# A two-layer diffusion trunk: the modulation sums of one stage moved to VectorE alone and cut into pieces of 512 columns

## The chip, the cores and the metric

One core of one Trainium2 chip. The metric is the device time of one execution in microseconds (us), the median of several runs. The whole program is one launch.

## The reference

Two layers of one trunk over 512 latent tokens (x) and 256 context tokens (ctx), 1024 channels wide. Each layer is a half step of SwiGLU, a token mixer, and a second half step of SwiGLU; each of the three is modulated by vectors that come from a conditioning vector c (for the latents) or c_ctx (for the context). Cut to what matters here:

```python
sc, scc = silu(c), silu(c_ctx)                       # 1024 numbers each
for li in range(2):
    m  = split(sc  @ ada_w[li] + ada_b[li], 9)       # nine vectors of 1024 for the latents
    mc = split(scc @ ada_w[li] + ada_b[li], 9)       # nine for the context
    h  = half_ffn(h,  norm_g[li, 0], m[0],  m[1],  m[2],  ffn_w_gu[li, 0], ffn_w_down[li, 0])
    hc = half_ffn(hc, norm_g[li, 0], mc[0], mc[1], mc[2], ffn_w_gu[li, 0], ffn_w_down[li, 0])
    ...
```

with half_ffn(h, g, shift, scale, gate, w_gu, w_down) = h + 0.5 * gate * swiglu(rms_norm(h, g) * (1 + scale) + shift). The part in question is the product of the two rows sc and scc with ada_w[1], a matrix of 1024 x 9216: the eighteen vectors of layer 1.

## The kernel before, in words

Activations lie transposed, channels on the 128 partitions: h is eight chunks (KC = 8) of 128 channels by 768 tokens. Every matrix product runs on TensorE in fp32r, with weights and activations split into a high and a low part (names ending in h and l) and three matmuls for each product. The stages follow one another: first half step of layer 0, even mixer, second half step of layer 0, first half step of layer 1, odd mixer, second half step of layer 1.

A half step (ffn, line 913) goes through 22 chunks of 128 hidden channels. For a chunk, chain (line 658) multiplies gate and up weights with all channels, for the 512 latent tokens and then for the 256 context tokens, into PSUM banks gb; ScalarE takes the silu (sg), VectorE multiplies (a<-sg,gb), and a is split into a high part (a cast, on ScalarE as a rule) and a low part (a<-a,a on VectorE). After every second chunk comes a down block (out_block, line 672): it multiplies the two chunks with the down weights into bank_c, bank_d and bank_e in turn, and for each of eight output chunks VectorE adds the result to h (h<-bank_c,mod,h). So the second half step of layer 0 is a row of gate/up stretches of two chunks with down blocks between them. Weights come by DMA into raw and are split: the high part w0h to w3h on ScalarE or VectorE, the low part w0l to w3l on VectorE or GpSimd, by whoever is free in the plan.

The modulation vectors of layer 1 are made beside that stage (class Ada, line 839). For one of nine vectors and for each kc of eight, 128 rows by 1024 columns of ada_w are loaded into araw (three buffers; the next load is put on SyncE's queue when the plan has the buffer read). Each row is scaled by its element of silu(c) or silu(c_ctx), a number for each partition, and added into aacc, of 2 x 1024 columns, one half for each of the two. In job (line 859) VectorE does the first half by itself, one scalar_tensor_tensor of 1024 columns; for the second half ScalarE forms the product (amul) and GpSimd adds it. Then sixteen small fp32 matmuls on TensorE against pick, the row sums, add up the 128 partitions of aacc into bank_f, and finish (line 885) copies them out (asb), transposes them with TensorE and adds ada_b into mods. aacc has one buffer, so that the next vector can't begin before the row sums have read it.

What sets the order. Each engine runs its instructions in the order in which the program issues them, and a planner decides this order when the program is built. It keeps a clock for each engine (Machine), which an instruction moves ahead by a cost formula (line 156): for VectorE 67 + 1.17 n ns for a scalar_tensor_tensor over n columns, for GpSimd 100 + 2.2 n. Side jobs are generators on lanes n, m, s, t, a, b and g; what a job yields is the time from which its next part may be issued, a number of ns from the plan's present, or sched.at(...) (line 218): when the named tiles are ready, less slack, and not before the clock of an engine, less lead. The present is TensorE's clock. Between groups of matmuls, tick (line 255) issues all parts whose time has come. In the down blocks of this stage tick is called for the lanes n and m alone, except with the last part (line 684). The modulation jobs run on lane b, from the start of the stage:

```python
for v in range(9):
    sch.add("b", ada.job(1, v, ADA_GAP), 6000.0)     # line 1794; ADA_GAP = 2500.0
```

After each kc job waits ADA_GAP ns, and before each it waits for VectorE's clock to have come to the present. Ahead of chunk 19 of 22 (line 947) the plan waits until lane b is empty, since the space of aacc is lent to weights from there on:

```python
if both and (kind, i) == ("gu", NFF - 3):
    sch.wait_for(lambda: not sch.lanes["b"])
```

The same job runs with seven vectors of layer 0 in the very first stage; the change doesn't touch those.

Of the kernel before, what the change touches and what calls it, by code (L numbers as in the profile page):

```python
# [7 lines left out]
F32 = mybir.dt.float32  # L8
# [3 lines left out]
ALU = mybir.AluOpType  # L12
AXX = mybir.AxisListType.X

D = 1024
KC = 8
# [13 lines left out]
ADA_GAP = 2500.0  # L30
# [34 lines left out]
class Machine:  # L65
# [23 lines left out]
    def rows(self, ap):  # L89

        name = ap.tensor.name
        if name not in self.mem:
            rows, key = [], getattr(ap.tensor, "cap_key", None)
            if key is not None:
                past = self.past.setdefault(key, [])
                bufs = ap.tensor.tag_meta.bufs or 1
                if len(past) >= bufs:
                    rows.append([0, 1 << 30, 0, 128, 0.0, "", self.last(past[-bufs])])
                past.append(name)
            self.mem[name] = rows  # L100
        if ap.space != bass.MemoryType.SB:
            return self.mem[name], (0, 1 << 30, 0, 128)
        step, parts = ap.ap[0]
        p0, lo = divmod(ap.offset, step) if step else (0, ap.offset)
        hi = lo + 1
        for st, n in ap.ap[1:]:
            if st > 0:
                hi += st * (n - 1)
            else:
                lo += st * (n - 1)  # L110
        return self.mem[name], (lo, hi, p0, p0 + parts)
# [196 lines left out]
def trunk(ctx, tc, t, out, stop=None, dbg=None):  # L308
    nc = Machine(tc.nc)
    sch = Sched(nc)  # L310
# [14 lines left out]
    st = const.tile([128, KC, 32], F32, name="st")  # L325
# [513 lines left out]
    class Ada:  # L839
# [11 lines left out]
        def load(self):  # L851
            if self.at < len(self.todo):
# [3 lines left out]
                nc.sync.dma_start(out=raw, in_=t["ada_w"][li, 128 * kc:128 * kc + 128, D * vec:D * vec + D])  # L856
                self.raws.append(raw)

        def job(self, li, vec, gap):

            acc = self.pool.tile([128, 2, D], F32, tag="aacc", name="aacc")
            for kc in range(KC):
                while not self.raws:
                    yield 100.0
                yield sch.at(self.raws[:1], eng="dve")
                raw = self.raws.pop(0)
                s0, s1 = st[:, kc, 0:1], st[:, kc, 1:2]
                if kc == 0:
                    nc.vector.tensor_scalar_mul(acc[:, 0], raw, s0)
                    nc.scalar.mul(acc[:, 1], raw, s1)  # L870
                else:
                    nc.vector.scalar_tensor_tensor(out=acc[:, 0], in0=raw, scalar=s0, in1=acc[:, 0], op0=ALU.mult, op1=ALU.add)
                    m = self.pool.tile([128, D], F32, tag="amul", name="amul", bufs=1)
                    nc.scalar.mul(m, raw, s1)
                    nc.gpsimd.tensor_tensor(out=acc[:, 1], in0=acc[:, 1], in1=m, op=ALU.add)
                sch.later(sch.at([], [raw]), self.load)
                yield gap
            yield sch.at([acc])
            for v in range(2):
                for j in range(4):  # L880
                    nc.tensor.matmul(bank_f[32 * j:32 * j + 32, 0:256], pick[:, v], acc[:, v, 256 * j:256 * j + 256],
                                     start=(v == 0), stop=(v == 1))
            yield from self.finish(li, vec)
# [295 lines left out]
    def ffn_alloc(pool):  # L1179
        def alloc(kind, grp, k=0):  # L1180
            t0, n, _ = grp
            if kind in ("acc", "pen", "last"):
                return pool.tile([128, n], F32, tag=f"{kind}{t0}", name=kind)
            if kind == "rs":
                return pool.tile([128, n], F32, tag=f"rs{t0}", name=kind)
            if kind == "u":
                return pool.tile([128, D], F32, tag="araw", name="u", bufs=3)[:, 0:n]
            return pool.tile([128, TX], F32, tag="sq", name=kind, bufs=3)[:, 0:n]
        return alloc
# [5 lines left out]
    def ffn_rooms():  # L1195
        return {0: (bank_e, bank_f[:, 0:16]), 512: (gb[3], bank_f[:, 16:32])}


    with tc.manual_schedule():
# [15 lines left out]
        ada = Ada(fp, [(0, (2, 3, 4, 5, 6, 7, 8))], 3)  # L1215
# [575 lines left out]
        ada = Ada(fp, [(1, tuple(range(9)))], 3)  # L1791
        ada.fill()
        for v in range(9):
            sch.add("b", ada.job(1, v, ADA_GAP), 6000.0)
        n3 = Norm(1, 0, ffn_alloc(fp), ffn_rooms())
        ffn(fp, gb, 0, 1, [XG, CG], n3, early)
        if stop == "ffn01":
# [360 lines left out]
```

## Time and profile before

| | |
|---|---|
| median of three runs | 2685.04 us (2680.67 to 2686.91) |
| the profiled execution, its own time | 2681.97 us |
| its span, first to last instruction | 2680.2 us |
| mean granted TensorE clock | 0.987 of full speed |
| TensorE matmuls, busy | 2596.9 us, 97% of the span |
| VectorE busy | 1858.7 us, 69% |
| ScalarE busy | 824.9 us, 31% |
| GpSimd busy | 737.9 us, 28% |
| DMA | 249.33 MB, mean 93 GB/s |

The times of engines are from one execution, by the hardware profiler. PE is TensorE (PEld its weight loads), DVE VectorE, ACT ScalarE, POOL GpSimd, SP SyncE, which issues most DMAs. In a row of the timeline stand the start and the length in us, the engine, the line, the operation, the tile written and those read, and a count where several were merged; in brackets the idle time of the engine ahead of it and what ended that. All instructions carry line 198, that of a helper, so that tiles tell them apart. Matmuls are pipelined: one shown with 0.39 us may start 0.23 us behind the last.

### The profile page before, as it was taken

The page shows a single profiled execution, that of the slowest core. Times are in us where ns is not written, and L with a number is a line of the kernel's source. Part 1 is how long each engine was busy: PE and PEld are TensorE (multiplying, and loading weights), DVE is VectorE, ACT ScalarE, POOL GpSimd, SP SyncE. Part 2 cuts the span into 40 slices and gives each one's busy share as a digit, 9 for nine tenths or more (in the row PEclk, how much of TensorE's full clock was granted, in tenths as well). Part 3 has the DMA queues.
Part 4 walks back from the last instruction along what each step waited for, and adds up shares of the span by engine and source line. Part 5 has one row for each costly group of instructions (what it writes and reads, how often), then busy time and mean ns, then how long its engine had stood idle before and what let it go on. Part 6 is the DMA issues. An engine that isn't in the chain of part 4 may idle for free.

```text
span 2680.2 us, 38122 instructions
## 1 busy us (share of the span) xinstructions
PE 2596.9 (97%) x15498; PEld 2254.8 (84%) x15498; DVE 1858.7 (69%) x2727; ACT 824.9 (31%) x1365; POOL 737.9 (28%) x481
## 2 busy tenths in 40 slices
PE   7999999999999889999999999999999999899999
PEld 6888888888777678888888889999997887888887
DVE  6888875456666677788875688787876667655554
ACT  4332321123434432332331433232334333311111
POOL 2453541013433342444441201010113443200000
PEclk9999999999999989999999999999998999899999
DMA  9544542212111144444442113121321212233332
GB/s 270 150 149 126 157 134 63 71 48 79 35 34 27 48 134 125 146 147 133 142 144 68 56 32 95 56 87 48 92 73 36 68 53 66 63 95 95 95 95 87
DMA packets 286922, 249.33 MB, mean 93 GB/s; under 512 B 26178, under 2 KB 256026, under 8 KB 286746
## 3 DMA queue, kind: packets, MB, share of 16 engines
q1 hardware_dynamic: 286378, 246.81, 31.2%
q8 instruction: 121, 1.98, 0.3%
q14 instruction: 55, 0.45, 0.1%
q10 hardware_dynamic: 176, 0.07, 0.0%
q0 software_dynamic: 192, 0.01, 0.0%
HBM read 244.73 MB, written 2.13 MB: 92 GB/s over the span
## 4 chain that ended last, share of the span: by engine, by line
PE 88%; DVE 6%; ACT 2%; issue 1%; DMA 1%; POOL 1%; SPq 0%; ACTq 0%; DVEq 0%; POOLq 0%
PE gb L198 46%; PE bank_c L198 14%; PE bank_d L198 13%; PE bank_e L198 10%; PE bank_f L198 3%; PE S L198 1%; DVE a L198 1%; DVE zl L198 1%; PE Sx L198 1%; PE TB L198 1%; DVE h L198 0%; DVE aacc L198 0%; SPq L198 0%; ACT zh L198 0%; POOL aacc L198 0%
## 5 line engine op out<-in xcount | busy, mean ns | idle before, releaser
L198 POOL TENSOR_TENSOR aacc<-aacc,amul 128x1024 f32<-128x1024 f32 x112 | 309.3, 2762 | 298.8 <-ACT amul L198 287.3
L198 DVE TENSOR_TENSOR a<-sg,gb 128x512 f32<-128x512 f32 (+1 forms) x112 | 64.0, 572 | 303.1 <-PE gb L198 302.6
L198 DVE SCALAR_TENSOR_TENSOR aacc<-araw,st,aacc 128x1024 f32<-128x1024 f32 x112 | 234.1, 2091 | 2.2 <-DMA araw<-in_ada_w 0.2
L198 DVE SCALAR_TENSOR_TENSOR h<-bank_c,mod,h 128x512 f32<-128x512 f32 (+1 forms) x237 | 151.0, 637 | 70.6 <-PE bank_c L198 70.3
L198 DVE SCALAR_TENSOR_TENSOR h<-bank_d,mod,h 128x512 f32<-128x512 f32 (+1 forms) x234 | 148.8, 636 | 69.8 <-PE bank_d L198 69.4
L198 PE MATMUL gb<-zh,w1h 128*128 128x512 f32 (+2 forms) x520 | 175.3, 345 | 0.0
L198 ACT ACTIVATE amul<-araw,st 128x1024 f32<-128x1024 f32 x112 | 128.8, 1150 | 148.1 <-POOL aacc L198 130.6
L198 PE MATMUL gb<-zh,w1l 128*128 128x512 f32 (+2 forms) x512 | 171.7, 342 | 0.0
L198 PE MATMUL gb<-zh,w3h 128*128 128x512 f32 (+2 forms) x504 | 169.0, 344 | 0.0
L198 PE MATMUL gb<-zl,w1h 128*128 128x512 f32 (+2 forms) x488 | 167.2, 343 | 0.0
L198 PE MATMUL gb<-zh,w0l 128*128 128x512 f32 (+2 forms) x496 | 165.4, 343 | 0.0
L198 PE MATMUL gb<-zh,w2l 128*128 128x512 f32 (+2 forms) x488 | 162.9, 344 | 0.0
L198 PE MATMUL gb<-zh,w3l 128*128 128x512 f32 (+2 forms) x480 | 162.2, 344 | 0.0
L198 PE MATMUL gb<-zl,w3h 128*128 128x512 f32 (+2 forms) x468 | 161.1, 344 | 0.0
L198 PE MATMUL gb<-zh,w0h 128*128 128x512 f32 (+2 forms) x472 | 160.9, 348 | 0.0
L198 PE MATMUL gb<-zh,w2h 128*128 128x512 f32 (+2 forms) x472 | 159.5, 346 | 0.0
L198 PE MATMUL gb<-zl,w0h 128*128 128x512 f32 (+2 forms) x444 | 153.5, 346 | 0.1
L198 ACT CAST a<-a 128x512 fp32r<-128x512 f32 (+1 forms) x115 | 61.1, 532 | 295.2 <-DVE a L198 295.0
L198 PE MATMUL gb<-zl,w2h 128*128 128x512 f32 (+2 forms) x440 | 151.8, 345 | 0.0
L198 DVE SCALAR_TENSOR_TENSOR h<-bank_e,mod,h 128x512 f32<-128x512 f32 (+1 forms) x185 | 117.6, 636 | 47.2 <-PE bank_e L198 47.2
L198 ACT ACTIVATE sg<-gb 128x512 f32<-128x512 f32 (+1 forms) x112 | 56.3, 502 | 283.1 <-PE gb L198 283.1
L198 POOL TENSOR_TENSOR u<-u,p 128x384 f32<-128x384 f32 x19 | 23.7, 1250 | 426.1 <-ACT p L198 426.1
(685 smaller groups left out, 7255.7 us busy)
## 6 DMA issues: line engine op xcount, KB each, us to landing
raw<-in_ffn_w_gu SPq DMA_DIRECT2D x176, 512.0 KB, 4.1
araw<-in_ada_w SPq DMA_DIRECT2D x134, 512.0 KB, 3.8
raw<-in_ffn_w_down SPq DMA_DIRECT2D x88, 512.0 KB, 3.7
raw<-in_od_w_in SPq DMA_DIRECT2D x16, 512.0 KB, 4.1
raw<-in_ev_w_in SPq DMA_DIRECT2D x10, 512.0 KB, 3.8
raw<-in_od_w_out SPq DMA_DIRECT2D x8, 512.0 KB, 3.8
xt<-in_ada_w SPq DMA_DIRECT2D x6, 512.0 KB, 7.3
xt<-in_x SPq DMA_DIRECT2D x4, 512.0 KB, 5.4
```

What stands on the lines that cost most here:

```text
L198: return real(*args, **kw)
```

## The change

Class Ada gets a second generator, own, and the row sums at the end of job become a generator of their own, rows, which both use. In own VectorE sums both halves of aacc, in pieces of 512 columns, four for each kc: the scalar for each partition times araw, added to aacc (for kc = 0 the product alone). After each piece the job yields until VectorE's clock in the plan is less than 600 ns ahead; the wait ahead of each kc has a lead of 300 ns; the gap behind each kc is 0.6 x 2500 = 1500 ns. The row sums are issued when the plan's end of the sums lies 2000 ns back (slack = -2000). The nine jobs of layer 1 use own; those of layer 0 keep job.

```diff
+        def own(self, li, vec, gap):
+
+            acc = self.pool.tile([128, 2, D], F32, tag="aacc", name="aacc")
+            for kc in range(KC):
+                while not self.raws:
+                    yield 100.0
+                yield sch.at(self.raws[:1], eng="dve", lead=300.0)
+                raw = self.raws.pop(0)
+                for v in range(2):
+                    for half in (slice(0, D // 2), slice(D // 2, D)):
+                        s1, o, i = st[:, kc, v:v + 1], acc[:, v, half], raw[:, half]
+                        if kc == 0:
+                            nc.vector.tensor_scalar_mul(o, i, s1)
+                        else:
+                            nc.vector.scalar_tensor_tensor(out=o, in0=i, scalar=s1, in1=o, op0=ALU.mult, op1=ALU.add)
+                        yield sch.at([], eng="dve", lead=600.0)
+                sch.later(sch.at([], [raw]), self.load)
+                yield gap
+            yield sch.at([acc], slack=-2000.0)
+            yield from self.rows(li, vec, acc)
+
         def job(self, li, vec, gap):
...
             yield sch.at([acc])
+            yield from self.rows(li, vec, acc)
+
+        def rows(self, li, vec, acc):
             for v in range(2):
                 for j in range(4):
                     nc.tensor.matmul(bank_f[32 * j:32 * j + 32, 0:256], pick[:, v], acc[:, v, 256 * j:256 * j + 256],
...
         for v in range(9):
-            sch.add("b", ada.job(1, v, ADA_GAP), 6000.0)
+            sch.add("b", ada.own(1, v, 0.6 * ADA_GAP), 6000.0)
```

## Rows read from the trace of the kernel before

**Rows 1.** Table of stretches: us, busy PE, PEld, DVE, ACT, POOL; clock, DMA share, GB/s

```profile
934.00:1450.00 516.00, 502.67 (x2943) 435.41 (x2942) 402.29 (x417) 158.20 (x200) 212.03 (x83) 0.98 0.43 132
...
960.00:1000.00 40.00, 32.78 (x191) 27.82 (x190) 30.88 (x25) 10.62 (x14) 17.85 (x7) 0.87 0.51 152
...
987.50:993.50 6.00, 5.82 (x28) 3.95 (x29) 0.99 (x4) 0.00 (x0) 0.00 (x0) 0.50 0.70 223
```

**Rows 2.** Waits of PE from 948 to 1434 us: total us, times, longest

```profile
PE bank_f L198 <- issue: 7.2, 1, 7.2
PE bank_d L198 <- DVE h L198: 3.3, 2, 1.7
PE bank_e L198 <- DVE h L198: 1.6, 1, 1.6
```

**Rows 3.** Timeline of PE around the first row sums

```profile
980.08 0.39 PE L198 MATMUL gb<-zh,w3l 128*128 128x512 f32 x1
987.68 1.93 PE L198 MATMUL bank_f<-aacc,pick 128*32 128x256 f32 x16 [7.22 <-issue]
```

**Rows 4.** Timelines of PE and DVE: later row sums, the next vector's first product

```profile
1170.99 1.07 PE L198 MATMUL bank_f<-aacc,pick 128*32 128x256 f32 x16
...
1175.17 2.74 DVE L198 TENSOR_SCALAR aacc<-araw,st 128x1024 f32<-128x1024 f32 x1
```

**Rows 5.** Timelines of DVE, POOL and PE at the start of a down block

```profile
1152.21 4.59 DVE L198 TENSOR_TENSOR a<-a,a 128x512 fp32r<-128x512 f32 x2
...
1153.76 2.76 POOL L198 TENSOR_TENSOR w0l<-raw,w0h 128x1024 fp32r<-128x1024 f32 x1
...
1155.03 0.61 PE L198 MATMUL bank_d<-a,w3h 128*128 128x512 f32 x2
1155.48 0.39 PE L198 MATMUL bank_d<-a,w3l 128*128 128x512 f32 x1
1157.52 0.73 PE L198 MATMUL bank_e<-a,w1h 128*128 128x512 f32 x2 [1.65 <-DVE h L198]
```

**Rows 6.** Timeline of DVE up to the first row sums

```profile
952.15 0.75 DVE L198 TENSOR_SCALAR aacc<-araw,st 128x1024 f32<-128x1024 f32 x1 [1.17 <-DMA araw<-in_ada_w]
...
963.01 8.07 DVE L198 SCALAR_TENSOR_TENSOR aacc<-araw,st,aacc 128x1024 f32<-128x1024 f32 x3
...
986.20 1.27 DVE L198 SCALAR_TENSOR_TENSOR aacc<-araw,st,aacc 128x1024 f32<-128x1024 f32 x1
```

**Rows 7.** Groups of instructions, 934 to 1450 us: busy us, mean ns, idle before

```profile
L198 DVE SCALAR_TENSOR_TENSOR aacc<-araw,st,aacc 128x1024 f32<-128x1024 f32 x63 | 131.4, 2086 | 1.1
L198 DVE TENSOR_TENSOR w1l<-raw,w1h 128x1024 fp32r<-128x1024 f32 x13 | 24.2, 1862 | 0.0
L198 DVE TENSOR_TENSOR a<-a,a 128x512 fp32r<-128x512 f32 x20 | 23.6, 1179 | 2.1 <-ACT a L198 2.1
...
L198 DVE TENSOR_SCALAR aacc<-araw,st 128x1024 f32<-128x1024 f32 x9 | 12.7, 1412 | 1.2 <-DMA araw<-in_ada_w 1.2
...
L198 ACT ACTIVATE amul<-araw,st 128x1024 f32<-128x1024 f32 x63 | 72.4, 1150 | 81.7 <-POOL aacc L198 72.8 <-DMA araw<-in_ada_w 8.9
...
L198 POOL TENSOR_TENSOR aacc<-aacc,amul 128x1024 f32<-128x1024 f32 x63 | 171.5, 2722 | 177.5 <-ACT amul L198 177.5
```

**Rows 8.** Timeline of DVE, instructions of 512 and 1024 columns with POOL idle

```profile
1001.07 0.75 DVE L198 SCALAR_TENSOR_TENSOR h<-bank_e,mod,h 128x512 f32<-128x512 f32 x1 [0.33 <-PE bank_e L198]
...
1034.75 0.68 DVE L198 TENSOR_TENSOR a<-a,a 128x512 fp32r<-128x512 f32 x1
1035.35 1.22 DVE L198 TENSOR_TENSOR w3l<-raw,w3h 128x1024 fp32r<-128x1024 f32 x1
1036.49 1.21 DVE L198 TENSOR_TENSOR w1l<-raw,w1h 128x1024 fp32r<-128x1024 f32 x1
```

**Rows 9.** Table of one stretch: all instructions, then those of aacc alone

```profile
1170.20:1205.00 34.80, 34.80 (x213) 30.06 (x212) 28.85 (x24) 13.04 (x16) 19.85 (x8) 1.00 0.54 166
...
1170.20:1205.00 34.80, 1.07 (x16) 0.42 (x16) 15.28 (x8) 1.15 (x1) 17.45 (x7) 1.00 0.54 166
```

## The prediction

> **What bounds the kernel now.** I read first the table of stretches for the second half step of layer 0, the only place where the change acts [rows 1]. It lasts from about 934 to 1450 us, and TensorE counts as busy for 502.7 of those 516 us; VectorE for 402.3, GpSimd for 212.0, ScalarE for 158.2. So TensorE bounds the step, and only what makes it wait, or run at a lower clock, can be won. Between 960 and 1000 us it is busy for 32.8 of 40 us at a mean granted clock of 0.87; that is where to look.
>
> The table of TensorE's waits between the start of the modulation sums and their end names three places [rows 2]: one wait of 7.2 us before a matmul into bank_f, and three of about 1.6 us on VectorE's update of h. The timeline of TensorE shows the first [rows 3]: the last matmul before it starts at 980.08, and the sixteen row sums of the first vector start at 987.68. [...] What was late? VectorE's last sum into aacc begins at 986.20 and takes 1.27 us, and 0.2 us behind its end the row sums begin [rows 6]. GpSimd isn't the last one here. VectorE is late because it is slow: the sum that takes 1.27 us by itself stands in a run of three that takes 8.07 us [rows 6]. Over the whole step 63 of them average 2.09 us [rows 7], while GpSimd's own additions, 63 of 2.72 us, read two operands from SBUF at the same time. The bystanders suffer as well: a<-a,a of 512 columns averages 1.18 us against 0.68 in a quiet moment, w1l 1.86 against 1.21 [rows 7, 8]. The three small waits are the same disease: two subtractions into a take 4.59 us beside GpSimd, the h updates behind them come late, and TensorE's next matmul starts 2.04 us after its predecessor instead of 0.23 [rows 5].
>
> **The change, part by part.** The profiled execution took 2681.97 us (span 2680.2), 3.1 us under the median of the three runs; I make the sum against it and put the forecast between the two.
>
> Removed: GpSimd's 63 additions (171.5 us) and ScalarE's 63 products (72.4 us), the nine first ones too [rows 7]. Neither engine ends a wait of TensorE in this table [rows 2], so by itself this is worth nothing; what counts is that VectorE has no company any more in its own sums and those around them. GpSimd keeps some of the weights' low parts, as the 2.76 us of w0l at 1153.76 [rows 5], and beside those VectorE stays slow.
>
> Added: the sums for c_ctx (the second half of aacc) on VectorE, and all of them in pieces. For VectorE a step was one instruction of 1024 columns; it is now four of 512. The trace has no such piece. From below: 512 columns with two SBUF operands start 0.60 us apart (1034.75 to 1035.35), less than that excludes itself, as the new instruction does more [rows 8]. From above: the h update of 512 columns, of the same operation but with one operand in PSUM, takes 0.75 [rows 8]. I take 0.67, half of 1.27 and a little, because the operand memories are those of the 1024-column row. The nine first steps multiply only (1024 columns in 0.75 us, undisturbed [rows 6]): 0.42 a piece, between 0.37 and 0.47. A vector is then 28 x 0.67 + 4 x 0.42 = 20.4 us, nine are 184 us, against 131.4 + 12.7 = 144.1 now [rows 7]: VectorE gets 40 us more. It gets back 20 x 0.50 = 10 us on a and 13 x 0.65 = 8 us on w1l [rows 7, 8], and similar sums on the other parts of the weights, so its busy time stays near 400 of 516 us. The cover for those 40 us is TensorE's own work. I cost them at nothing as long as a vector fits into one gate/up stretch, which is the real question of this case.
>
> [...]
>
> **Does a vector fit?** Lane b, on which the sums run, is served only in gate/up stretches (the down blocks serve lanes n and m alone, line 684), so order is decided by what fits between two down blocks. Take the stretch from 1170.2 to 1205.0, 34.8 us, VectorE busy 28.85, of which 15.28 for aacc [rows 9]. The other 13.6 us shrink without GpSimd's additions beside them by an estimated 4 us (a, w1l and a cast, at their quiet prices), to 9.5. The row sums of the vector before start at 1170.99, the next vector's first product at 1175.17 [rows 4]: 4.2 us of opening plus 0.8 before it, in which some 3 us of the 9.5 find room. So 5.0 + 20.4 + 6.5 = 31.9 of 34.8 us: eight steps fit, with 2.9 us or one step to spare. The shorter gap (1500 ns instead of 2500) and the leads (300 and 600 ns ahead of VectorE's planned end) matter for just this; a step's planned 4 x 666 ns (line 183) outlasts the gap, so VectorE is kept fed. There are nine stretches for nine vectors before line 947, where everything on lane b must be out.
>
> The margin: row sums are put in TensorE's order when the planner's end of the sums is 2 us past. For vectors that end with their stretch this is free, as a down block lies between (1155.03 to 1170.99 is 16 us [rows 4, 5]). For the first one it works against the 7.4 us. There VectorE's real start waits for the load of araw until 952.15, idle for 1.2 us [rows 6]; from there 20.4 us of its own and an estimated 10 of other work (as in the stretch above) end near 982.5, and TensorE, planned 2 us behind, gets there at about the same time. I leave 1 us of that wait. Each araw load on SP's queue now waits for VectorE alone and no longer for ScalarE's product too; the weight loads behind it on that queue go no later.
>
> The sum. First row sums: 987.68 - 980.08 - 0.23 = 7.4 us of standing, and at the low clock 0.9 us on the row sums plus half of some 3.4 us of matmuls up to 993.5, 1.7: 10.0 us. Three waits on h, 1.8 us each: 5.4 us. Together 15.4 won. Back go 1 us at the first row sums and, since a piece or two may now lie ahead of the first h update of a down block, an estimated 0.2 us in each of eight: 1.6. Net 12.8: 2681.97 - 12.8 = 2669.2; with 3.1 more for the median 2672.3; I say 2670.5.
>
> **Rivals.** One: a stretch holds only seven steps, because a piece costs 0.75 (28 x 0.08 = 2.2 us more) or the waits of the plan eat the spare step. Then one step is left over in each of eight stretches, and at line 947 TensorE stands until VectorE has made up 8 x 2.7 = 21.4 us, plus one opening of 4.2 and some 2.9 at half clock: 28.5 - 12.8 = 15.7 slower, about 2700. It decides from about three steps left (3 x 2.7 + 7.1 = 15.2). For it: one spare step is little. Against it: the order before fits its eight steps (x8 for aacc [rows 9]) with VectorE slowed. Chance 0.14.
>
> Two: the waits move instead of going. VectorE carries 40 us more of sums, and each down block then begins with an h update that stands behind pieces: 9 x 1.2 us, and the first row sums keep 3 us: 13.8 of the 15.4, next to nothing won, 2683. For it: the down blocks turn over three banks only, and GpSimd's low parts of weights still slow VectorE there. Against it: the pieces are a third of what now blocks (0.67 against 2.09 on average [rows 7], and more beside GpSimd). Chance 0.12.
>
> Three: the first row sums are cured, the three waits on h aren't: 2681.97 - 9.0 + up to 3.1, or 2673 to 2676; inside the forecast's range, 0.14. That GpSimd still slows VectorE as before, because the low parts move to it in numbers, is part of the second.
>
> **How the numbers follow.** The forecast, 2670.5, has 0.56 (with the third rival 0.70); 0.04 is left for what I don't see. A measurement of this kernel can tell 0.2%, 5.4 us, from no change. Faster: 0.70 and part of the second rival and the rest, 0.73; same: 0.12; slower: 0.15. The range goes from 2664 (all 15.4 us won, and a run as low as the lowest of before) to 2685, which takes in the second rival; above it lies the first.
>
> **What would show it.** Right: no wait over 3 us before the first row sums, no 0.50 stretch of clock behind them, pieces near 0.67 us, GpSimd busy under 50 us in the step, nine row sums of which most stand at the start of a stretch. Wrong: row sums and VectorE pieces crowded together at about 1430 us with TensorE idle (rival one); TensorE waiting for h at many down blocks (rival two).

## The result and the profile after

The changed kernel takes **2669.94 us** (median of 6 runs, 2665.57 to 2674.24), the kernel before, run beside it, 2682.89 us (6 runs, 2679.10 to 2686.91). The ratio is 0.9946, 95% interval 0.9936 to 0.9957: faster by 0.43 to 0.64%. The profiled execution after took 2669.66 us, with a span of 2667.5.

The table of stretches after, the same three stretches as in [rows 1]:

```profile
934.00:1450.00 516.00, 513.73 (x2999) 445.51 (x3000) 415.63 (x649) 83.97 (x135) 23.88 (x15) 0.99 0.45 135
960.00:1000.00 40.00, 40.00 (x235) 34.58 (x234) 34.88 (x56) 6.33 (x11) 0.00 (x0) 1.00 0.51 147
987.50:993.50 6.00, 6.00 (x54) 5.11 (x54) 2.96 (x9) 0.49 (x2) 0.00 (x0) 1.00 0.22 79
```

TensorE is busy for 11 us more of the same 516. Between 960 and 1000 us it doesn't stand at all, at a granted clock of 1.00 in place of 0.87, and the 0.50 around 990 us is gone. GpSimd went from 212.0 to 23.9 us and ScalarE from 158.2 to 84.0; VectorE rose by 13.3, to 415.6. Of the three rows of waits in [rows 2] none is left. Behind the start of the sums the table of TensorE's waits after has one row, for the copy that follows the last row sums, which stood there before as well:

```profile
PE bank_f L198 <- DVE asb L198: 0.5, 1, 0.5
```

The first row sums after, in the timelines of VectorE and TensorE, against [rows 3, 6]:

```profile
983.16 2.75 DVE L198 SCALAR_TENSOR_TENSOR aacc<-araw,st,aacc 128x512 f32<-128x512 f32 x4
...
988.41 0.28 PE L198 MATMUL gb<-zh,w3l 128*128 128x256 f32 x1
988.62 1.07 PE L198 MATMUL bank_f<-aacc,pick 128*32 128x256 f32 x16
```

VectorE's last four pieces end at 985.91, and TensorE gets to the row sums 2.7 us later, without a pause and at a granted clock of 1.00 in place of 0.50 (sixteen in 1.07 us, not 1.93). The groups of VectorE in the step after, against [rows 7]:

```profile
L198 DVE SCALAR_TENSOR_TENSOR aacc<-araw,st,aacc 128x512 f32<-128x512 f32 x252 | 172.3, 749 | 0.1
L198 DVE TENSOR_TENSOR w1l<-raw,w1h 128x1024 fp32r<-128x1024 f32 x15 | 23.9, 1592 | 0.0
L198 DVE TENSOR_SCALAR aacc<-araw,st 128x512 f32<-128x512 f32 x36 | 15.0, 479 | 1.0 <-DMA araw<-in_ada_w 1.0
L198 DVE TENSOR_TENSOR a<-a,a 128x512 fp32r<-128x512 f32 x20 | 13.7, 687 | 2.1 <-ACT a L198 2.1
```

A busy time over a count shows that neighbours overlap: 172.3 / 252 is 0.68 us a piece, though one shows 0.749. Twice as many columns are summed in 187 us as before in 144. The bystander a<-a,a is back at 0.69 from 1.18 us.

**Where the time came from.** To keep what happens ahead of the stage out, I pair two matmuls that are the same in both programs: the last one that waits for zl, ahead of the sums, and the one behind the ninth row sums. TensorE's timeline before, then after:

```profile
938.51 0.79 PE L198 MATMUL bank_c<-zl,w1h 128*128 128x512 f32 x1 [0.57 <-DVE zl L198]
...
1433.05 0.44 PE L198 MATMUL bank_f<-ident,asb 128*128 128x128 f32 x2 [0.55 <-DVE asb L198]
```

```profile
942.09 0.79 PE L198 MATMUL bank_c<-zl,w1h 128*128 128x512 f32 x1 [0.57 <-DVE zl L198]
...
1420.91 0.44 PE L198 MATMUL bank_f<-ident,asb 128*128 128x128 f32 x2 [0.55 <-DVE asb L198]
```

The stage took 494.54 us before and takes 478.82 after: 15.7 us won. The profiled execution after reached it 3.6 us later, though the two programs are the same up to there; the difference arises in the first 65 us. So the spans differ by 12.7 only.

### The profile page after: what moved, and what is told of

Its sections match the earlier page's. It is cut to its first block, busy times and chain, and to the rows that moved or that the text cites. A ratio compares the mean times of both kernels' runs of the same rounds, so it can differ in the third digit from the quotient of the medians.

```text
span 2667.5 us, 38131 instructions
## 1 busy us (share of the span) xinstructions
PE 2591.3 (97%) x15498; PEld 2252.1 (84%) x15498; DVE 1861.1 (70%) x2949; ACT 747.7 (28%) x1294; POOL 548.2 (21%) x411
## 4 chain that ended last, share of the span: by engine, by line
PE 90%; DVE 5%; ACT 2%; DMA 1%; issue 1%; POOL 1%; SPq 0%; ACTq 0%; POOLq 0%; DVEq 0%
PE gb L198 47%; PE bank_c L198 14%; PE bank_d L198 13%; PE bank_e L198 10%; PE bank_f L198 3%; PE S L198 1%; DVE zl L198 1%; PE Sx L198 1%; DVE a L198 1%; PE TB L198 1%; DVE h L198 0%; SPq L198 0%; DMA xt<-in_ada_w 0%; ACT zh L198 0%; DVE w2l L198 0%
## 5 line engine op out<-in xcount | busy, mean ns | idle before, releaser
L198 DVE SCALAR_TENSOR_TENSOR aacc<-araw,st,aacc 128x512 f32<-128x512 f32 (+1 forms) x301 | 271.4, 956 | 1.2 <-DMA araw<-in_ada_w 0.2
L198 POOL TENSOR_TENSOR aacc<-aacc,amul 128x1024 f32<-128x1024 f32 x49 | 137.7, 2811 | 126.9 <-ACT amul L198 125.6
L198 POOL TENSOR_TENSOR u<-u,p 128x384 f32<-128x384 f32 x19 | 23.9, 1258 | 425.5 <-ACT p L198 425.5
L198 PEld LDWEIGHTS gb<-zh,w1h 128*128 128x128 f32 x520 | 98.1, 189 | 11.5 <-issue 1.6
```

The source lines that it names most:

```text
L198: return real(*args, **kw)
```

## The experiments

My theory: VectorE was slow because GpSimd's additions read SBUF at the same time; taking those away is the whole of the gain. Rivals: the margin does it (the row sums were only placed too early), or the cut does it (h gets in between shorter pieces), or VectorE simply had too much to do. Each of the twelve runs is given by its median and by its ratio to the kernel before, timed beside it (medians 2685.24, 2686.29, 2684.80 and 2686.81 us in the four groups); ratios are what to compare between groups.

### The margin alone, of 2 and of 12 us

Kernel before, with

```diff
-            yield sch.at([acc])
+            yield sch.at([acc], slack=-2000.0 if li else 0.0)
```

and the same with -12000.0.

> The kernel before, with the margin alone: row sums of layer 1 put into TensorE's order 2 us later in the plan; VectorE, ScalarE and GpSimd share the sums as before. If GpSimd's additions beside VectorE are the cause, the first row sums still wait some 5.5 of 7.4 us, the clock still falls behind them, and the three waits on h stay: 1.5 to 3 us won, about 2680. If the missing margin is the cause, the first wait goes with its 10 us: about 2673.

> The kernel before with a margin of 12 us in the plan, more than any delay seen. Both theories let the first wait go (10 us won). If GpSimd's additions are the cause, the three waits on h of 1.8 us stay, 2673; if all waits come from row sums planned too early, they go as well, 2668.

The 2 us margin: 2684.61 us, ratio 0.9999 (0.9989 to 1.0008). The 12 us margin: 2677.02, 0.9975 (0.9964 to 0.9985). The waits of TensorE in the stage, with 2 us, then with 12 us:

```profile
PE bank_f L198 <- issue: 5.5, 1, 5.5
PE bank_d L198 <- DVE h L198: 5.0, 3, 1.7
PE bank_e L198 <- DVE h L198: 1.6, 1, 1.6
```

```profile
PE bank_d L198 <- DVE h L198: 5.0, 3, 1.7
PE bank_e L198 <- DVE h L198: 1.7, 1, 1.7
```

With 2 us the first wait shrinks by 1.7 us, as it should, but row sums now stand elsewhere in the later stretches and a fourth wait on h appears, of 1.65: nothing is left of the gain. With 12 us the first wait is gone altogether, and with it the low clock behind it (1.00 from 1000 to 1012 us, where the first row sums now stand); the four waits on h stay. So the first loss is a matter of placing and can be cured by it. The waits on h can't. Timelines of VectorE, then GpSimd, at the new one (2 us margin):

```profile
1100.26 4.60 DVE L198 TENSOR_TENSOR a<-a,a 128x512 fp32r<-128x512 f32 x2
1104.78 0.74 DVE L198 SCALAR_TENSOR_TENSOR h<-bank_d,mod,h 128x512 f32<-128x512 f32 x1
...
1099.38 2.41 POOL L198 TENSOR_TENSOR aacc<-aacc,amul 128x1024 f32<-128x1024 f32 x1 [1.27 <-ACT amul L198]
1101.82 2.76 POOL L198 TENSOR_TENSOR w1l<-raw,w1h 128x1024 fp32r<-128x1024 f32 x1
```

The two subtractions, one of 512 columns and one of 256 (a merged row shows the shape of its first), last from 1100.26 to 1104.86, and GpSimd's two instructions from 1099.38 to 1104.58; h waits behind them.

### GpSimd's additions left out

Kernel before, layer 1:

```diff
-                    nc.gpsimd.tensor_tensor(out=acc[:, 1], in0=acc[:, 1], in1=m, op=ALU.add)
+                    if li:
+                        nc.run("pool", 100.0 + 2.2 * D, [acc[:, 1], m], [acc[:, 1]])
```

> The kernel before with GpSimd's 63 additions into the second half of aacc left out (the context's vectors of layer 1 are then incomplete); the plan still counts their time, so that the order of everything else is the same, and ScalarE still forms the products. If GpSimd's additions slow VectorE, its sums of 1024 columns average about 1.3 instead of 2.09 us, all four waits of TensorE go: 15 us won, 2667 to 2669. If VectorE is late from its own load or from ScalarE, the waits stay: 2681 to 2684.

2668.99 us, ratio 0.9944 (0.9924 to 0.9963), as fast as the changed kernel. No margin, no cut, VectorE with its old share, and all four losses are gone. Its group of sums, and the pair of subtractions of [rows 5], in VectorE's timeline:

```profile
L198 DVE SCALAR_TENSOR_TENSOR aacc<-araw,st,aacc 128x1024 f32<-128x1024 f32 x63 | 80.8, 1282 | 11.7 <-DMA araw<-in_ada_w 10.8
```

```profile
1144.10 1.02 DVE L198 TENSOR_TENSOR a<-a,a 128x512 fp32r<-128x512 f32 x2
1145.76 0.75 DVE L198 SCALAR_TENSOR_TENSOR h<-bank_e,mod,h 128x512 f32<-128x512 f32 x1 [0.64 <-PE bank_e L198]
```

The same 63 sums take 80.8 us instead of 131.4, 1.28 each instead of 2.09, and the pair 1.02 instead of 4.59; VectorE now waits for TensorE there and not the other way round. ScalarE still forms its products (161.2 us busy in the step), so it isn't the disturber. This shows the cause. That VectorE had too much to do falls: the changed kernel gives it 100 us more than this one (415.6 against 313.9 busy) and is no slower.

### Parts of the change taken back

Changed kernel without the margin, and with whole rows of 1024 columns:

```diff
-            yield sch.at([acc], slack=-2000.0)
+            yield sch.at([acc])
```

```diff
-                    for half in (slice(0, D // 2), slice(D // 2, D)):
+                    for half in (slice(0, D),):
```

> The changed kernel without its margin (slack 0). If VectorE without company is what counts, its plan is true by itself: the first row sums wait 1.5 us at most, 2669 to 2672. If the margin counts, 5 us or more of the first wait are back with the low clock: 2676 to 2680.

> The changed kernel with pieces of 1024 columns, two for each kc, instead of four of 512. If company was the cause, the cut matters little: 2668 to 2672, no wait on h over 1 us. If the size of the blocks was the cause of the waits on h, they are back in some down blocks, 5 us or more: 2675 or above.

2670.77 and 2670.79 us, both 0.9954 (0.9938 to 0.9970): neither part by itself is worth anything that can be measured. Both were then taken back together:

> The changed kernel without two of its three extras: pieces of 1024 columns, no margin; what stays is VectorE alone with 1.5 us between steps. My theory now (the waits came from VectorE and GpSimd reading SBUF at the same time, and from nothing else): 2670 to 2672, no wait over 3 us before the first row sums, none on h at a down block. Rival (cut and margin each cover for the other, which is why leaving out one alone showed nothing): a wait of 3 to 10 us before the first row sums, or waits on h of 0.7 to 1.3 us as a 1024-column piece now stands in front of h; 2674 to 2681.

2667.83 us, 0.9933 (0.9915 to 0.9951). The rival, that each covers for the other, falls: in this stage no wait of TensorE stands in the table at all, not even the half microsecond for asb, as the ninth row sums come a stretch earlier. Its sums:

```profile
L198 DVE SCALAR_TENSOR_TENSOR aacc<-araw,st,aacc 128x1024 f32<-128x1024 f32 x126 | 155.2, 1277 | 2.4 <-DMA araw<-in_ada_w 2.1
```

By busy time a whole row takes 155.2 / 126 = 1.23 us, and two pieces take 2 x 172.3 / 252 = 1.37: a cut costs 0.14 us, some 19 us of VectorE over the step with the first products (187.3 against 155.2 + 12.7), and buys nothing here. The prediction's prices, 0.67 a piece and 1.27 a row, make it 2 x 0.67 - 1.27 = 0.07, half of the measured 0.14; its 0.67 was an estimate, half of 1.27 and a little.

### The cut alone

Kernel before, with VectorE's own half of the sums in two pieces of 512 columns in layer 1:

```diff
-                    nc.vector.scalar_tensor_tensor(out=acc[:, 0], in0=raw, scalar=s0, in1=acc[:, 0], op0=ALU.mult, op1=ALU.add)
+                    for c in ((slice(0, D // 2), slice(D // 2, D)) if li else (slice(0, D),)):
+                        nc.vector.scalar_tensor_tensor(out=acc[:, 0, c], in0=raw[:, c], scalar=s0, in1=acc[:, 0, c], op0=ALU.mult, op1=ALU.add)
```

> The kernel before with VectorE's own half of the sums of layer 1 cut into pieces of 512 columns; ScalarE and GpSimd do the other half as before. If company is the cause, the pieces are slowed as the whole was and the waits stay: 2680 to 2685. If the size of VectorE's blocks is the cause, the three waits on h go: 2677 or less.

2681.90 us, 0.9985 (0.9976 to 0.9995). The group of sums, then TensorE's waits:

```profile
L198 DVE SCALAR_TENSOR_TENSOR aacc<-araw,st,aacc 128x512 f32<-128x512 f32 x126 | 145.8, 1214 | 0.3
```

```profile
PE bank_f L198 <- issue: 8.3, 1, 8.3
PE bank_d L198 <- DVE h L198: 1.3, 3, 0.6
...
PE bank_e L198 <- DVE h L198: 0.3, 1, 0.3
```

Less is lost on h, 1.6 us in four waits against 4.9 in three, so that I was wrong to expect these waits to stay. But h doesn't get in between pieces: in front of it stand the subtractions into a, as before. Timelines of VectorE, then GpSimd, at one of the four:

```profile
1158.28 3.23 DVE L198 TENSOR_TENSOR a<-a,a 128x512 fp32r<-128x512 f32 x2
1161.44 0.73 DVE L198 SCALAR_TENSOR_TENSOR h<-bank_e,mod,h 128x512 f32<-128x512 f32 x1
...
1158.76 2.47 POOL L198 TENSOR_TENSOR aacc<-aacc,amul 128x1024 f32<-128x1024 f32 x1 [3.86 <-ACT amul L198]
```

In this run's order GpSimd's addition begins only when most of the first subtraction is done: the subtractions of 512 columns average 0.72 us here, near the undisturbed 0.68, those of 256 still 0.92, so that it is the one of 256 that is held up, and the pair takes 3.23 us, not the 4.59 of [rows 5]. Meanwhile a piece of 512 shows 1.21 us beside GpSimd, and the sums take 145.8 instead of 131.4, so the first vector comes later still, 8.3 us against 7.2. The cut eases one symptom and feeds the other.

### The gap between steps

The changed kernel with 2500 ns between steps, as the old job had, then 2000 and 1000, in place of 1500:

```diff
-            sch.add("b", ada.own(1, v, 0.6 * ADA_GAP), 6000.0)
+            sch.add("b", ada.own(1, v, ADA_GAP), 6000.0)
```

(0.8 * ADA_GAP and 0.4 * ADA_GAP in the others.)

> The changed kernel with the gap behind each kc at 2500 ns as before, instead of 1500. If it takes the shorter gap to fit a vector into a gate/up stretch (the first rival of the prediction), steps are left over where lane b has to be empty, and TensorE stands there for about 2.7 us each: one step a stretch is 8 x 2.7 + 7 = 28 us, so 2690 to 2705. If the gap is hidden behind VectorE's own time, nothing changes: 2668 to 2672.

> The changed kernel with 2.0 us between the steps in place of 1.5 (it was 2.5 in the run that lost 40 us, where some 14 of the 72 steps were left when the last h was done). If the steps flow over the ends of the stretches, a step costs 2.7 + 2.0 = 4.7 us of the about 34 us that a stretch gave at 2.5 (6.5 steps of 5.2), so 7.2 steps each, 7 left at the end: 7 x 2.7 = 19 us without matmuls and about 3 at the low clock, 2690 to 2695. If only whole steps count (seven in a stretch): nine left, 24 + 5, 2696 to 2700. If a stretch has the room that I read off before (31.9 of 34.8 us at 1.5, so 2.9 spare against 8 x 0.5 = 4 more): one or two steps left, 2673 to 2676.

> The changed kernel with 1.0 us between the steps in place of 1.5. Theory: the stretch then has 4 us to spare and the row sums come earlier; nothing else hangs on the gap, so 2669 to 2671, the same as at 1.5. Rival (the gap protects VectorE's other work: zl, h and a of the blocks, and the weight pieces, which then queue behind four pieces of 0.67): waits on h or on a weight piece of 1 to 2 us at some of the eight down blocks, 2674 to 2685.

2500 ns: **2710.08 us**, 1.0089 (1.0069 to 1.0108), slower than before and beyond what I had expected. 2000: 2670.33, 0.9945 (0.9928 to 0.9962). 1000: 2668.43, 0.9938 (0.9914 to 0.9961). At 2500 ns the row sums of the last two vectors stand at the end, with TensorE idle ahead of each, and the table of that stretch shows the clock:

```profile
1434.78 3.06 PE L198 MATMUL bank_f<-aacc,pick 128*32 128x256 f32 x16 [15.83 <-DVE aacc L198]
...
1457.49 3.06 PE L198 MATMUL bank_f<-aacc,pick 128*32 128x256 f32 x16 [18.69 <-DVE aacc L198]
```

```profile
1421.00:1457.50 36.50, 3.50 (x20) 0.97 (x20) 34.77 (x58) 0.45 (x1) 0.00 (x0) 0.55 0.58 173
```

TensorE stands for 15.83 + 18.69 = 34.5 us, and each set of sixteen row sums takes 3.06 us instead of 1.07. The low clock, 0.50 from 1434.5 to 1438.0 us, is only part of that (at 0.50 the sixteen of [rows 3] took 1.93): the rest fits the pace of VectorE's last pieces, 34.6 / 52 = 0.67 us apart, for which the row sums wait. The 56 pieces that VectorE does there are 14 of the 72 steps: by the timeline most of the nine stretches did six steps (8, 7, 6, 6, 6, 6, 6, 7, 6). Yet VectorE was not full. One stretch at 2500 ns, then the same one of the changed kernel, all instructions and those of aacc alone:

```profile
1163.10:1197.80 34.70, 34.70 (x213) 30.20 (x212) 25.67 (x41) 4.36 (x8) 0.00 (x0) 1.00 0.44 137
```

```profile
1162.20:1196.80 34.60, 34.60 (x211) 29.90 (x210) 31.03 (x48) 4.17 (x8) 2.38 (x1) 1.00 0.58 173
...
1162.20:1196.80 34.60, 1.07 (x16) 0.42 (x16) 20.73 (x32) 0.00 (x0) 0.00 (x0) 1.00 0.58 173
```

At 2500 ns VectorE is busy for 25.67 of 34.7 us and could have taken more; the plan held it back. At 1500 and at 2000 every stretch from the third on does its eight steps. So the gap is what the gain hangs on, with an edge between 2000 and 2500 ns. Below the edge no difference can be measured; the rival of the last run, that a short gap lets pieces block h, falls.

### The same in layer 0

The kernel before loses 4.4 us in the first half step as well, in the waits of TensorE from 60 to 600 us:

```profile
PE bank_c L198 <- DVE h L198: 4.4, 3, 2.1
```

The changed kernel, with six of layer 0's seven vectors by VectorE alone:

```diff
-        gated = [sch.add("b", ada.job(0, v, 0.0 if v == 2 else ADA_GAP)) for v in range(2, 9)][0]
+        gated = [sch.add("b", ada.job(0, v, 0.0) if v == 2 else ada.own(0, v, 0.6 * ADA_GAP)) for v in range(2, 9)][0]
```

> The changed kernel with the same treatment for six of the seven vectors of layer 0 in the first half step (all but the first, which the first down block waits for). There TensorE has two waits on h, at about 250 and 407 us, of 2.3 and 2.0 us more than the pitch of its matmuls. If they have the same cause they go: about 4 us won, 2665 to 2667. If they don't, 2669 to 2671.

2664.91 us, 0.9926 (0.9907 to 0.9944), and that row is gone; the interval still overlaps that of the changed kernel. Last, the same with whole rows and without the margin:

> The best of both: the second half step's vectors by VectorE alone in whole pieces and without the margin, and six of layer 0's seven as well (GpSimd keeps its half of one). In the run that carried the change into layer 0 the two waits of the first half step (2.1 and 1.8 us before the down blocks near 253 and 409 us) went and the time fell to 2664.9; without cut and margin the second half step was 2.6 us shorter than in the changed kernel. Theory (the one cause, both parts independent): 2662 to 2664. Rival (in layer 0, where the steps share VectorE with other work, whole pieces of 1.28 us stand in front of h or a again): one or both of the two waits come back, 2665 to 2668.

**2658.89 us**, 0.9896 (0.9881 to 0.9911), faster than both kernels: its interval lies below that of the changed one. The waits on h stay away in both half steps, and the whole rows show 1.279 us with no loss:

```profile
L198 DVE SCALAR_TENSOR_TENSOR aacc<-araw,st,aacc 128x1024 f32<-128x1024 f32 x126 | 155.4, 1279 | 2.3 <-DMA araw<-in_ada_w 2.3
```

That is 3 us under the lower end of what I expected, though its profiled execution took 2662.72. Whether cut and margin cost those few microseconds stays open: the two intervals, of this run and the run before, overlap a little.

## Why the prediction was right

The forecast was 2670.5 us and faster; 2669.94 was measured. Step by step:

- **The cause**, GpSimd's additions beside VectorE's sums, is shown by the run without the additions. Of the waits it named, all four went.
- **What is won**, 15.4 us, was right: 15.7 between the paired matmuls. The first row sums gave 9.9, forecast 10.0 (its 0.9 us is 1.93 - 1.07 [rows 3, 4], its half of 3.4 us comes from the clock of 0.50 up to 993.5 us [rows 1], its 0.23 from the starts in [rows 5]); the three waits on h gave 1.95 each when such pairs are followed through the stage, not 1.8.
- **What was given back** was the mis-sized term: 1 us at the first row sums and 0.2 in each of eight down blocks, 2.6 together. Both are nothing. The row sums wait for nothing at all, since VectorE ends 2.7 us ahead (at 985.91; I had it at 982.5 with TensorE just behind), and no down block has a wait on h. The net of 12.8 us beside a difference of spans of 12.7 is therefore luck in part: 15.7 were won in the stage, and the execution after had come to it 3.6 us late. Over all runs the ratio says 14.5 us, between 11.5 and 17.2, which takes in both 12.8 and 15.7.
- **The price of a piece**, 0.67 us, is 0.68 by busy time, but the price of a cut in it, 0.07, was 0.14: a whole row in a row of them takes 1.23, not 1.27. A first piece 15.0 / 36 = 0.42 as said. A vector's 20.4 us are 20.73 in the stretch shown, 31.03 of 34.6 with the rest, where I had 31.9 of 34.8 with the opening counted in.
- **VectorE's load** was to stay near 400 us and went to 415.6. The sums cost 43 us more (187.3 against 144.1), where I had 40, and 19 of them are the cut; a gave back 9.9 of the forecast 10; w1l gave back next to nothing of its 8 (24.2 to 23.9 us, for 15 instead of 13). The mean of w1l is two prices mixed, as the section below shows. VectorE isn't the bound, so this cost nothing.
- **The margin and the cut** were costed as parts that help; neither is needed, as the runs without them show. The change's own additions to the plan are thus one that decides, the gap, and two that do nothing here.
- **Rival one**, that a stretch holds too few steps, did not happen here, but its mechanism is real: at the old gap six steps fit, 14 are left over, and the time is 2710. I had said that the planned 4 x 666 ns outlast the gap, so that VectorE is kept fed; at 2500 ns they outlast it too, and VectorE stands still a quarter of the stretch. The error is in how the program counts: the gap begins only when less than 600 ns of the last piece are left, so that pieces and gap add up. By the plan's own costs (an estimate, as no run shows the plan) a step takes some 4 x 666 - 600 ns and the gap, and eight of them 28.5 us at 1500, 32.5 at 2000 and 36.5 at 2500, in a stretch of 34.6: the edge lies where the runs have it. The spare room was also more than the 2.9 us read off: 2000 ns adds eight times 0.5 and still fits, where all three of my cases for it had steps left over. **Rival two**, that waits move instead of going, is what the 2 us margin alone does. **Rival three**, the first row sums cured and not h, is the 12 us margin: I had 2673 to 2676, it took 2677.0.

## What to carry to other kernels

When an engine's instruction shows a mean well above what the same instruction takes in a quiet moment, look for the engine that works beside it then, before moving work about (here GpSimd's additions took the sums from 1.28 to 2.09 us; ScalarE's products, beside them in the run with 1.28, were not the cause): giving the slowed engine the disturber's work too can be the faster split, and here it was, at 13 us more of its busy time for twice the sums. Try the placing alone and the cut alone as well: each moved the waits without shortening the kernel by more than a quarter per cent. And where a plan spaces work out, change the spacing together with the work's size; one such number was worth 40 us here.

## What the runs showed that was not expected

In these rows VectorE and GpSimd do not run side by side at a lower rate: the one that begins second does nearly all its work when the first has ended. A timeline of VectorE, then of GpSimd, in the changed kernel:

```profile
1164.24 2.62 DVE L198 TENSOR_TENSOR w1l<-raw,w1h 128x1024 fp32r<-128x1024 f32 x1
...
1163.39 2.38 POOL L198 TENSOR_TENSOR w3l<-raw,w3h 128x1024 fp32r<-128x1024 f32 x1 [49.06 <-DVE w3h L198]
```

GpSimd ends at 1165.77, and VectorE's instruction, which takes 1.22 us by itself, ends at 1166.86: it was begun in the middle of GpSimd's and did nearly all its work in the 1.09 us behind it. Of the step's w1l, those that meet a w3l on GpSimd show 2.62 us and the others 1.22 or 1.23. In the run without margin the plan happens to give GpSimd no w3l, and all fifteen are quick:

```profile
L198 DVE TENSOR_TENSOR w1l<-raw,w1h 128x1024 fp32r<-128x1024 f32 x15 | 18.2, 1215 | 0.0
```

Other starts come out alike. In the kernel before, w1l is begun 0.14, 1.51 and 1.86 us into a GpSimd instruction (at 958.55, 1003.78 and 1105.13); it takes 3.41, 1.97 and 1.62 us and ends 1.08 us behind GpSimd's each time. It also holds the other way round. Timelines of VectorE, then GpSimd, in the kernel before:

```profile
1068.04 1.22 DVE L198 TENSOR_TENSOR w1l<-raw,w1h 128x1024 fp32r<-128x1024 f32 x1
1069.17 3.42 DVE L198 TENSOR_TENSOR w3l<-raw,w3h 128x1024 fp32r<-128x1024 f32 x1
...
1068.79 2.71 POOL L198 TENSOR_TENSOR aacc<-aacc,amul 128x1024 f32<-128x1024 f32 x1 [22.65 <-ACT amul L198]
```

VectorE is first here and keeps its 1.22 us; GpSimd's addition takes 2.71 us, where the shortest of its kind takes 2.39, and VectorE's next instruction again ends 1.09 us behind it.

Not every instruction of VectorE is held. Timelines of VectorE, then GpSimd, in the kernel before:

```profile
1003.11 0.75 DVE L198 SCALAR_TENSOR_TENSOR h<-bank_d,mod,h 128x512 f32<-128x512 f32 x1 [0.61 <-PE bank_d L198]
1003.78 1.97 DVE L198 TENSOR_TENSOR w1l<-raw,w1h 128x1024 fp32r<-128x1024 f32 x1
...
1002.27 2.40 POOL L198 TENSOR_TENSOR w3l<-raw,w3h 128x1024 fp32r<-128x1024 f32 x1 [2.19 <-ACT w3h L198]
```

The update of h, with one operand in a PSUM bank, begins 0.84 us into GpSimd's instruction and keeps the 0.75 us of [rows 8]; w1l, with both operands in SBUF, begins next and takes 1.97 us, not the 1.21 of [rows 8]. That fits the SBUF of my theory; why one waits for the other there, no run shows. The price in a mixed stage is 2.09 us on average, not 1.28, for a sum of 1024 columns and 1.18, not 0.69, for a subtraction of 512. Such a mean hides two prices: of the twenty subtractions of 512 columns before, fourteen take 0.68 or 0.69 us and six between 2.02 and 2.90.
